# Moving fifteen modulation weight tiles from GpSimd to VectorE and TensorE

## The chip, the cores and the metric

The kernel runs on one core of a Trainium2 chip. The core's engines each work through their own instruction list: TensorE (PE in the profile; its weight loads are the row PEld), VectorE (DVE), ScalarE (ACT) and GpSimd (POOL); SyncE (SP) issues transfers. They meet at semaphores. The metric is the device time of one execution in microseconds (us), as the median of several runs.

## What is computed

One encoder block on 256 tokens of width 1024, in float32: a mixer of two kinds of attention and then a retrieval of experts, each between a norm with modulation and a gate. Cut to what matters here:

```
c_act = silu(c)                                   # c: 1024 numbers
ada = c_act @ w_ada + b_ada                       # 1024 x 6144
shift1, scale1, gate1, shift2, scale2, gate2 = split(ada, 6)
h = rms_norm(x, norm1_g) * (1 + scale1) + shift1
proj = h @ w_in                                   # queries, keys, values of both groups
mixed = [rms_norm(windowed attention), rms_norm(neighbourhood attention)]
x = x + gate1 * (mixed @ w_out)
h2 = rms_norm(x, norm2_g) * (1 + scale2) + shift2
x = x + gate2 * peer(h2, w_query, sub_keys, u_experts, v_experts)
return rms_norm(x, final_g)
```

The six modulation vectors have 1024 entries each, and each entry is a sum over 1024 products of silu(c) with a column of w_ada.

## The kernel before

All channels lie on the partitions, eight chunks of 128, and the 256 tokens along the free dimension. The kernel has two large stages.

**The first stage** covers everything from the first norm to the first queries of the expert part. It is not written in the order in which it runs. Its code records jobs (`add`), each with one or more engines that could do it, a cost in microseconds for each, what it waits for, and the buffers that it takes and frees. `run_plan` at the end of the stage then searches 300 rounds for an order by these costs, and writes out one instruction list per engine from the best one. The search starts from a fixed seed (`SEED = 729`). So a different cost, or a job on another engine, can change the order of everything in the stage, and which engine does a job that has more than one alternative.

The jobs that matter here:

- `load` (L586): SyncE loads weight tiles of 128 x 1024 f32 one after another, in the order in which they are recorded, into nine early buffers and eight raw ones that are taken in turn. A transfer waits until its buffer has been freed.
- `load_ada` (L592): forty modulation tiles, eight chunks of 128 channels for each of scale1, shift1, gate1, shift2 and scale2. A tile holds the 128 output channels on its partitions and the 1024 inputs along its rows. For 25 of them VectorE multiplies the tile by silu(c), which lies on all partitions as `ca`, and sums each row in the same instruction (`scalar_tensor_tensor` with an accumulator, L606). For the 15 in `ON_POOL` GpSimd multiplies (L598) and ScalarE then sums the rows (L601). Gate2's eight tiles are read later, in the second stage.
- `load_w` (L614): a weight of the projections is split into a rounded high half (ScalarE) and a low half, the rest (`low`, L630: VectorE, or GpSimd as the second alternative, because `LO_POOL` is 1). Products with it are three passes (L442).
- attention units 0 to 7: scores on PE (L925, L927), bias and maximum on VectorE (L945), exponentials on ScalarE (L949), small additions for the sink (L962), multiplication by the reciprocal of the sum (L982: VectorE, ScalarE or GpSimd), transposes on PE (L999, L1002), copies of these (L1007 on VectorE, L1009 on ScalarE), the outputs on PE (L1021, L1025), scaling by the group norm's weight (L1032 VectorE, L1034 ScalarE). Evacuations of the input projection are L851 and L870.
- `op` (L540) is a helper for small elementwise jobs, so that many different ones carry that line; the low halves of activations (`hb`) are among them.
- the output projection in two groups of four weight tiles (first units 0 to 3, then 4 to 7), each followed by the gate (L1077) and the residual addition (L1081); then the second norm, and the early queries on PE (L1113).

**The second stage** has the rest of the queries, the top-k and the expert tables: products with the u table (L1507), then with the v table (L1557), and rows gathered by index (L1421) that VectorE multiplies and adds (L1443). Its tiles come through SyncE (L373) into the same raw buffers and others.

Of the kernel before, what the change touches and what calls it, by code (L numbers as in the profile page):

```python
# [12 lines left out]
AF = mybir.ActivationFunctionType  # L13
# [3 lines left out]
P = 128  # L17
D = 1024
NC8 = 8
# [16 lines left out]
NCST = _o  # L36

SHIFT1, SCALE1, GATE1, SHIFT2, SCALE2, GATE2 = range(6)
ON_POOL = {(GATE1, 0), (GATE1, 2), (GATE1, 3), (GATE1, 5), (GATE1, 7), (SCALE2, 0), (SCALE2, 1), (SCALE2, 2), (SCALE2, 4), (SCALE2, 5), (SCALE2, 6), (SHIFT2, 1), (SHIFT2, 2), (SHIFT2, 3), (SHIFT2, 4)}
RAW = 4  # L40
SETTLE = 6.0
SETS = (64, 32)
# [17 lines left out]
LO_POOL = 1  # L60
# [5 lines left out]
def kernel(ctx: ExitStack, tc: tile.TileContext, xT, crow, vecs, cst, w_ada, w_in, w_out,  # L66
# [78 lines left out]
    def add(alts, *deps, take=(), free=(), lag=0.0, after=None, rows=P):  # L145
        return Job(alts, deps, take, free, lag, after, rows)
# [174 lines left out]
    MM = 0.1095  # L321
# [16 lines left out]
    tiles = {}  # L338
# [178 lines left out]
    def silu(y, x):  # L517
        S.activation(y, x, AF.Exp, scale=-1.0)
        V.tensor_scalar(y, y, 1.0, None, op0=ALU.add)
        V.reciprocal(y, y)  # L520
        V.tensor_mul(y, y, x)

    silu(c8t[:8], c8[:8])
    for w, part in ((0, SCALE1), (1, SCALE2)):
        a0 = VEC["b_ada"][0] + part * 8
        V.scalar_tensor_tensor(gb[:, w, :], vec[:, a0:a0 + 8], 1.0, v_("g2" if w else "g1"),
                               op0=ALU.add, op1=ALU.mult)
# [64 lines left out]
    def load_ada(part, c):  # L592
        key = ("ada", part, c)
        m = load(w_ada[part, c], key)
        col = ada[:, part, c:c + 1]
        if (part, c) in ON_POOL:
            def mul():
                G.tensor_mul(tiles[key], tiles[key], ca)  # L598

            def total():  # L600
                S.activation(tiles[key], tiles[key], AF.Copy, accum_out=col)  # L601

            m = add([("pool", 2.3, mul)], m, *cas)
            column[part, c] = add([("act", 1.04, total)], m, free=[key])
        else:
            column[part, c] = add([("dve", 1.15, lambda: V.scalar_tensor_tensor(  # L606
                tiles[key], tiles[key], 1.0, ca, op0=ALU.mult, op1=ALU.mult, accum_out=col))], m, *cas, free=[key])

    halved = {}
# [4 lines left out]
    def load_w(kind, i):  # L614
        key = ("w", kind, i)
        m = load(SRC[kind][i], key)
        hkey = ("h", kind, i)
        held_key[kind, i] = hkey
        if (kind, i) in WHOLE or kind == "q" and i < NQ:
            halved[kind, i] = whole[kind, i] = m  # L620
            held_key[kind, i] = key
            return

        def high():
            halves[kind, i] = new_halves(got(hkey))
            S.activation(halves[kind, i][0], tiles[key].rearrange("p (c n) -> p c n", n=P), AF.Copy)

        def low(e):
            hi, lo = halves[kind, i]
            e.tensor_sub(lo, tiles[key].rearrange("p (c n) -> p c n", n=P), hi.bitcast(F32))  # L630

        a = add([("act", 0.95, high)], m, take=[("split", hkey)])
        halved[kind, i] = add([("dve", 1.14, lambda: low(V))] + [("pool", 2.3, lambda: low(G))] * LO_POOL, a, free=[key])


    lscr = dram.tile([8, 512], F32, name="lscr")
# [1001 lines left out]
def _layout(np, i):  # L1638
# [26 lines left out]
    for c in range(8 if KT == 16 else 0):  # L1665
# [5 lines left out]
    w_out = w_out.reshape(2, 4, P, 4, 2, P).transpose(0, 3, 2, 4, 1, 5).reshape(8, P, D)  # L1671
    rpb = np.stack([i["rpb_b"][0].reshape(4, 2, 465)[:, :, 108 + 31 * r:264 + 31 * r] for r in range(4)])
    rpb = rpb.transpose(2, 0, 1, 3).reshape(-1)
    return {
        "xT": i["x"][0].T.reshape(8, P, T).transpose(1, 0, 2),
        "crow": i["c"].reshape(8, P),
        "vecs": vec,
        "cst": _constants(np),
        "w_ada": i["w_ada"][0].T.reshape(6, 8, P, D),
        "w_in": w_in,  # L1680
        "w_out": w_out,
        "w_query": tiles(i["w_query"][0]),
# [27 lines left out]
```

## Time and profile before

| | |
|---|---|
| median of 3 runs | 851.04 us (849.75 to 851.42) |
| profiled execution | 850.8 us, of it 849.0 us between the first and the last instruction (the span) |
| PE busy | 775.2 us, 91% of the span |
| VectorE busy | 593.1 us, 70% |
| GpSimd busy | 330.6 us, 39% |
| ScalarE busy | 268.0 us, 32% |
| mean granted clock of TensorE | 0.976 |

A share over the whole span is an average over stages with different limits, so it does not say what sets the time of one of them. The rows below take the span in stretches: up to 61 us, to 141.5 and to 176.3 us lie in the first stage (61 us is the end of the products for the first twelve column blocks of the input projection, 141.5 us the beginning of the second half of the output projection, 176.3 us the end of the early queries), from 220 us the products with the u table, from 482.3 us those with the v table.

Names in the rows: `big`, `raw` and `vec` are areas in SBUF, `b` a PSUM bank, `xs` the residual, `hi`/`lo` the halves of a weight, `hb` the halves of activations, `in_...` tensors in memory.

### The profile page before, as it was taken

The page shows a single profiled execution, that of the slowest core. Times are in us where ns is not written, and L with a number is a line of the kernel's source. Part 1 is how long each engine was busy: PE and PEld are TensorE (multiplying, and loading weights), DVE is VectorE, ACT ScalarE, POOL GpSimd, SP SyncE. Part 2 cuts the span into 40 slices and gives each one's busy share as a digit, 9 for nine tenths or more (in the row PEclk, how much of TensorE's full clock was granted, in tenths as well). Part 3 has the DMA queues.
Part 4 walks back from the last instruction along what each step waited for, and adds up shares of the span by engine and source line. Part 5 has one row for each costly group of instructions (what it writes and reads, how often), then busy time and mean ns, then how long its engine had stood idle before and what let it go on. Part 6 is the DMA issues. An engine that isn't in the chain of part 4 may idle for free.

```text
span 849.0 us, 15375 instructions
## 1 busy us (share of the span) xinstructions
PE 775.2 (91%) x5846; PEld 753.9 (89%) x5846; DVE 593.1 (70%) x1308; ACT 268.0 (32%) x741; POOL 330.6 (39%) x271
## 2 busy tenths in 40 slices
PE   3998786789799999999999999999999989899894
PEld 1997575689799999999999999999999988899893
DVE  6999999887677999569998775644435444453534
ACT  4456675456231112179876521000000000000003
POOL 2545686456314436412233233533333333332300
PEclk9999998999999999999999999999999999999997
DMA  8995666095768999999999999999999999999951
GB/s 328 408 328 206 223 227 234 0 348 202 259 229 297 392 413 395 416 413 361 359 378 374 401 371 416 415 412 416 415 416 415 414 415 416 415 413 418 414 205 50
DMA packets 81212, 289.27 MB, mean 341 GB/s; under 512 B 9281, under 2 KB 10825, under 8 KB 81010
## 3 DMA queue, kind: packets, MB, share of 16 engines
q1 hardware_dynamic: 36352, 125.60, 38.5%
q0 software_dynamic: 27776, 100.79, 30.2%
q10 hardware_dynamic: 17010, 61.89, 18.4%
q8 instruction: 46, 0.75, 0.4%
q14 instruction: 28, 0.23, 0.1%
HBM read 287.18 MB, written 1.07 MB: 340 GB/s over the span
## 4 chain that ended last, share of the span: by engine, by line
PE 34%; DMA 28%; issue 5%; DVE 3%; POOL 3%; ACT 0%; DVEq 0%; ACTq 0%; POOLq 0%
PE b L1507 27%; DMA row<-in_vE,big 24%; PE b L1557 4%; DMA raw<-in_vE,big 3%; PE b L1474 2%; DVE accg L1443 1%; POOL row L1421 1%; DMA row<-in_uT 1%; POOL raw L1421 1%; DMA row<-in_vE 1%; PE b L1342 1%; PE b L1562 0%; POOL big L1421 0%; DVE big L1443 0%; POOL lo L398 0%
## 5 line engine op out<-in xcount | busy, mean ns | idle before, releaser
L1507 PE MATMUL b<-big 128*128 128x160 f32 x928 | 134.3, 302 | 4.0 <-ACT big L1489 4.0
L1557 PE MATMUL b<-big 128*128 128x160 f32 x944 | 131.0, 299 | 5.0 <-DMA big<-in_vE 4.2
L1557 PEld LDWEIGHTS b<-big 128*128 128x128 f32 x944 | 129.0, 190 | 5.7 <-DMA big<-in_vE 4.7
L1557 PE MATMUL b<-big,row 128*128 128x160 f32 x864 | 125.5, 305 | 7.4 <-DMA row<-in_vE 7.4
L1507 PEld LDWEIGHTS b<-big 128*128 128x128 f32 x928 | 128.4, 191 | 4.2 <-ACT big L1489 4.2
L1557 PEld LDWEIGHTS b<-big,row 128*128 128x128 f32 x864 | 121.8, 194 | 8.1 <-DMA row<-in_vE 4.3
L1507 PE MATMUL b<-big,row 128*128 128x160 f32 x752 | 106.6, 300 | 0.0
L1507 PEld LDWEIGHTS b<-big,row 128*128 128x128 f32 x752 | 103.0, 190 | 0.0
L540 ACT ACTIVATE big<-xs 128x256 f32<-128x256 f32 (+1 forms) x20 | 9.1, 457 | 283.8 <-DVE xs L540 273.8
L1421 POOL DMA_INDIRECT row<-in_vE,big x48 | 49.9, 1039 | 88.0 <-DVE accg L1443 58.5
L1443 DVE SCALAR_TENSOR_TENSOR accg<-row,big,accg 128x1024 f32<-128x1024 f32 x32 | 41.2, 1286 | 51.2 <-DMA row<-in_vE,big 48.4
L442 PE MATMUL b<-hb,hi 128*128 128x256 f32 x432 | 65.5, 295 | 1.9 <-DVE hb L540 1.9
L1421 POOL DMA_INDIRECT raw<-in_vE,big x36 | 37.2, 1033 | 70.5 <-DVE accg L1443 45.5
L1421 POOL DMA_INDIRECT row<-in_uE,big x37 | 39.6, 1071 | 61.9 <-DVE big L1493 29.2
L1489 ACT ACTIVATE big<-b 128x160 f32<-128x160 f32 (+23 forms) x110 | 29.0, 266 | 104.3 <-PE b L1507 85.4
L442 PEld LDWEIGHTS b<-hb,hi 128*128 128x128 f32 x432 | 58.2, 199 | 3.9 <-DVE hb L540 2.1
L1421 POOL DMA_INDIRECT raw<-in_uE,big x34 | 34.5, 1015 | 63.6 <-DVE raw L1434 29.0
L1443 DVE SCALAR_TENSOR_TENSOR accg<-raw,big,accg 128x1024 f32<-128x1024 f32 x23 | 29.6, 1285 | 38.2 <-DMA raw<-in_vE,big 38.1
L1465 ACT ACTIVATE oh<-iota,ebf 128x128 f16<-128x128 f16 x160 | 51.0, 394 | 13.2 <-PE b L1474 9.4
L1421 POOL DMA_INDIRECT big<-in_uE,big x25 | 25.7, 1028 | 70.1 <-issue 29.3
L442 PE MATMUL b<-hb,lo 128*128 128x256 f32 x216 | 33.1, 291 | 6.6 <-DVE lo L630 5.0
L442 PEld LDWEIGHTS b<-hb,lo 128*128 128x128 f32 x216 | 28.7, 194 | 8.6 <-DVE lo L630 5.6
(212 smaller groups left out, 1381.2 us busy)
## 6 DMA issues: line engine op xcount, KB each, us to landing
big<-in_uT SPq DMA_DIRECT2D x36, 512.0 KB
big<-in_w_ada SPq DMA_DIRECT2D x33, 512.0 KB
big<-in_vE SPq DMA_DIRECT2D x31, 512.0 KB
row<-in_vE SPq DMA_DIRECT2D x29, 512.0 KB
big<-in_vE ACTq DMA_DIRECT2D x28, 512.0 KB
row<-in_vE ACTq DMA_DIRECT2D x25, 512.0 KB
row<-in_uT ACTq DMA_DIRECT2D x24, 512.0 KB
row<-in_uT SPq DMA_DIRECT2D x23, 512.0 KB
```

Source lines behind the costliest of these rows:

```text
L442: PE.matmul(ps, w[:, wc, :], r[:, rc, :], start=(n == 0), stop=(n == last))
L540: return (e, cost, lambda: f(*a, **k))
L1342: PE.matmul(px[:, c * P:(c + 1) * P], rep[:, 4 * i + c, :], ident, start=True, stop=True)
L1421: G.indirect_dma_start(row, None, uE if k < GT else vE, bass.IndirectOffsetOnAxis(ap=cidx[:, k % GT:k % GT + 1], axis=0))
L1443: V.scalar_tensor_tensor(accg[w], row, ag[:, k - GT:k - GT + 1], accg[w], op0=ALU.mult, op1=ALU.add)
L1465: S.activation(oh1[:, k, :], iota1, AF.Square, scale=-1.0, bias=ebf[:, t0 + k:t0 + k + 1])
L1474: PE.matmul(pg[:, k, :], pr[:, i, :, k], oh1[:, k, :], start=(i == 0), stop=(i == 1))
L1489: S.activation(gz[:, e, t:], ps[:, 0, t:ND], AF.Gelu_apprx_tanh)
L1507: PE.matmul(ps[:, 0, 0:ND], w[:, c, :], h2[:, c, GT:], start=(c == 0), stop=(c == NC8 - 1))
L1557: PE.matmul(acc[c][:, 0, GT:], w[:, c, :], gz[:, e, :], start=(e == 0), stop=(e == NE - 1), skip_group_check=True)
```

## The change

The set `ON_POOL` and its branch go. Five of its fifteen tiles (four of scale2, one of shift2) are in a new set `ON_PE`. For them the host lays the tile out the other way, with 128 inputs on the partitions and eight blocks of 128 output channels; PE takes each block as the stationary operand and multiplies it by one column of silu(c) in column form (`cs`, made by a second `silu` at the start), eight matmuls that add up in one PSUM bank, and ScalarE copies the resulting column of 128 numbers to its place. These jobs wait for their tile's transfer and for a free bank. The other ten tiles fall into the branch for VectorE. Two costs of the planner are raised, 1.15 to 1.3 us for VectorE's sum and 1.14 to 1.22 for VectorE's low half. In the changed kernel most lines are one or two higher (L540 is L541, L630 is L632, L1081 is L1083), VectorE's sum is L608 and the new product L602.

```diff
@@ -36,7 +36,7 @@
-ON_POOL = {(GATE1, 0), (GATE1, 2), (GATE1, 3), (GATE1, 5), (GATE1, 7), (SCALE2, 0), (SCALE2, 1), (SCALE2, 2), (SCALE2, 4), (SCALE2, 5), (SCALE2, 6), (SHIFT2, 1), (SHIFT2, 2), (SHIFT2, 3), (SHIFT2, 4)}
+ON_PE = {(SCALE2, 0), (SCALE2, 2), (SCALE2, 4), (SCALE2, 6), (SHIFT2, 2)}
@@ -521,6 +521,7 @@
     silu(c8t[:8], c8[:8])
+    silu(cs, v_("c"))
@@ -593,17 +594,18 @@
         col = ada[:, part, c:c + 1]
-        if (part, c) in ON_POOL:
-            def mul():
-                G.tensor_mul(tiles[key], tiles[key], ca)
-
-            def total():
-                S.activation(tiles[key], tiles[key], AF.Copy, accum_out=col)
-
-            m = add([("pool", 2.3, mul)], m, *cas)
-            column[part, c] = add([("act", 1.04, total)], m, free=[key])
+        if (part, c) in ON_PE:
+            def products_c():
+                w = tiles[key].rearrange("p (c n) -> p c n", n=P)
+                pc = take_bank(("adac", part, c))
+                for k in range(NC8):
+                    PE.matmul(pc[:, 0, 0:1], w[:, k, :], cs[:, k:k + 1], start=(k == 0), stop=(k == NC8 - 1))
+
+            m = add([("pe", 16 * MM, products_c)], m, take=[("bank", ("adac", part, c))], free=[key])
+            column[part, c] = add([("act", 0.25, lambda: S.activation(
+                col, tiles["adac", part, c][:, 0, 0:1], AF.Copy))], m, free=[("adac", part, c)])
         else:
-            column[part, c] = add([("dve", 1.15, lambda: V.scalar_tensor_tensor(
+            column[part, c] = add([("dve", 1.3, lambda: V.scalar_tensor_tensor(
                 tiles[key], tiles[key], 1.0, ca, op0=ALU.mult, op1=ALU.mult, accum_out=col))], m, *cas, free=[key])
@@ -630,7 +632,7 @@
-        halved[kind, i] = add([("dve", 1.14, lambda: low(V))] + [("pool", 2.3, lambda: low(G))] * LO_POOL, a, free=[key])
+        halved[kind, i] = add([("dve", 1.22, lambda: low(V))] + [("pool", 2.3, lambda: low(G))] * LO_POOL, a, free=[key])
@@ -1671,12 +1673,15 @@
+    ada = i["w_ada"][0].T.reshape(6, 8, P, D).copy()
+    for part, c in ON_PE:
+        ada[part, c] = ada[part, c].T.reshape(8, P, P).transpose(1, 0, 2).reshape(P, D)
...
-        "w_ada": i["w_ada"][0].T.reshape(6, 8, P, D),
+        "w_ada": ada,
```

The order of the instructions is drawn up anew from the changed jobs. On GpSimd, in the middle of the first stage (L660 is the last step of the neighbourhood's bias; `raw_...` are buffers of the loads), stood before:

```order
L660 TENSOR_TENSOR big<-big 128x4x128 x3
L598 TENSOR_TENSOR big<-big 128x1024 x2
L598 TENSOR_TENSOR raw_667<-raw_667,big 128x1024
L598 TENSOR_TENSOR raw_724<-raw_724,big 128x1024
L598 TENSOR_TENSOR big<-big 128x1024
L982 TENSOR_TENSOR big<-big 128x2x256 x2
L598 TENSOR_TENSOR raw_884<-raw_884,big 128x1024
L598 TENSOR_TENSOR big<-big 128x1024 x3
L540 TENSOR_TENSOR big<-big 128x256
L982 TENSOR_TENSOR big<-big 128x2x256
```

and there stands after the change:

```order
L662 TENSOR_TENSOR big<-big 128x4x128 x3
L632 TENSOR_TENSOR lo_662<-big,hi_661 128x1024
L632 TENSOR_TENSOR lo_761<-raw_722,hi_760 128x1024
L632 TENSOR_TENSOR lo_888<-raw_818,hi_887 128x1024
L984 TENSOR_TENSOR big<-big 128x2x256
L632 TENSOR_TENSOR lo_977<-big,hi_976 128x1024
L541 TENSOR_TENSOR big<-big 128x256
L541 TENSOR_TENSOR hb<-big,hb 128x256
L541 TENSOR_TENSOR big<-big 128x256
L541 TENSOR_TENSOR hb<-big,hb 128x256 x2
```

The fifteen multiplications are gone from there, and four low halves stand in their place, with the weighing of attention weights (L982, now L984) later than before.

On PE, around the first attention units (`b_...` are PSUM banks, L442 products of the input projection, L862 and L999 transposes, L925 scores; `hi`, `lo` with a number the halves of one weight tile), stood before:

```order
L999 MATMUL b_824<-big 128x128 x4
L999 MATMUL b_833<-big 128x128 x4
L925 MATMUL b_841<-big 128x256
L925 MATMUL b_842<-big 128x256
L925 MATMUL b_841<-big 128x256
L925 MATMUL b_842<-big 128x256
L442 MATMUL b_858<-hb,hi_803 128x256 x8
L442 MATMUL b_858<-hb,lo_804 128x256 x8
L442 MATMUL b_858<-hb,hi_803 128x256 x8
L999 MATMUL b_899<-big 128x128 x4
L1021 MATMUL b_906<-big 64x256 x4
L442 MATMUL b_917<-hb,hi_853 128x256 x8
```

and now, around the first of the new products:

```order
L442 MATMUL b_862<-hb,hi_848 128x256 x8
L442 MATMUL b_862<-hb,lo_849 128x256 x8
L442 MATMUL b_862<-hb,hi_848 128x256 x8
L1001 MATMUL b_902<-big 128x128 x4
L602 MATMUL b_908<-cs,big 128x1 x8
L864 MATMUL b_930<-big 128x128 x4
L1001 MATMUL b_937<-big 128x128 x4
L927 MATMUL b_946<-big 128x256
L927 MATMUL b_947<-big 128x256
L927 MATMUL b_946<-big 128x256
L927 MATMUL b_947<-big 128x256
L1001 MATMUL b_962<-big 128x128 x4
```

The new product (L602) stands between the transposes of one unit and those before the scores of the next, and the products of the column blocks ahead of it come before the scores rather than after them.

On VectorE, in the second half of the output projection (L1077 gates, L1081 adds to the residual), stood before:

```order
L1081 TENSOR_TENSOR xs<-xs,big 128x256
L630 TENSOR_TENSOR lo_1408<-big,hi_1407 128x1024
L721 TENSOR_TENSOR big<-big 128x256
L715 TENSOR_SCALAR big<-b_1372 128x256
L724 TENSOR_TENSOR big<-big 128x256
L727 SCALAR_TENSOR_TENSOR big<-big 128x256
L1077 SCALAR_TENSOR_TENSOR big<-b_1381,ada,big 128x256
L1081 TENSOR_TENSOR xs<-xs,big 128x256
L1077 SCALAR_TENSOR_TENSOR big<-b_1426,ada,big 128x256
L1077 SCALAR_TENSOR_TENSOR big<-b_1381,ada,big 128x256
L1081 TENSOR_TENSOR xs<-xs,big 128x256 x2
L1077 SCALAR_TENSOR_TENSOR big<-b_1426,ada,big 128x256
```

and now (L1079 and L1083 are the same steps):

```order
L1079 SCALAR_TENSOR_TENSOR big<-b_1435,ada,big 128x256
L1083 TENSOR_TENSOR xs<-xs,big 128x256
L1079 SCALAR_TENSOR_TENSOR big<-b_1435,ada,big 128x256
L632 TENSOR_TENSOR lo_1494<-raw_1211,hi_1493 128x1024
L1079 SCALAR_TENSOR_TENSOR big<-b_1468,ada,big 128x256 x2
L1083 TENSOR_TENSOR xs<-xs,big 128x256 x2
L632 TENSOR_TENSOR lo_1533<-big,hi_1532 128x1024
L1079 SCALAR_TENSOR_TENSOR big<-b_1505,ada,big 128x256
L1083 TENSOR_TENSOR xs<-xs,big 128x256
L1079 SCALAR_TENSOR_TENSOR big<-b_1505,ada,big 128x256
L1083 TENSOR_TENSOR xs<-xs,big 128x256
L632 TENSOR_TENSOR lo_1570<-big,hi_1569 128x1024
```

Three low halves of weights now stand between the gates and the residual additions, where one stood before, ahead of the norm's steps (L715 to L727).

## Rows read from the trace of the kernel before

**Rows 1.** Stretches: length, busy us (instructions) per engine, PE clock, DMA share, GB/s.

```profile
0.00:61.00 61.00, 45.35 (x308) 42.15 (x308) 52.40 (x84) 29.17 (x46) 26.11 (x24) 1.00 0.95 359
61.00:141.50 80.50, 59.58 (x505) 50.01 (x503) 79.69 (x154) 53.05 (x140) 55.87 (x25) 0.95 0.66 233
141.50:176.30 34.80, 28.45 (x154) 25.47 (x155) 31.66 (x59) 17.83 (x40) 17.04 (x16) 0.84 0.20 67
220.00:482.30 262.30, 256.88 (x2045) 254.91 (x2044) 213.96 (x629) 121.02 (x400) 89.42 (x84) 0.99 0.95 366
482.30:797.00 314.70, 302.35 (x2217) 300.83 (x2216) 157.95 (x183) 15.15 (x52) 111.08 (x110) 0.99 1.02 411
```

**Rows 2.** VectorE's groups, 61 to 141.5 us: busy us, mean ns, idle before.

```profile
L606 DVE SCALAR_TENSOR_TENSOR raw<-raw,big 128x1024 f32<-128x1024 f32 x6 | 14.6, 2435 | 0.0
L630 DVE TENSOR_TENSOR lo<-raw,hi 128x1024 fp32r<-128x1024 f32 x7 | 13.3, 1903 | 0.0
...
L982 DVE TENSOR_TENSOR big<-big 128x512 f32<-128x512 f32 x9 | 9.7, 1085 | 0.2
L630 DVE TENSOR_TENSOR lo<-big,hi 128x1024 fp32r<-128x1024 f32 x4 | 7.1, 1768 | 0.0
L606 DVE SCALAR_TENSOR_TENSOR big<-big 128x1024 f32<-128x1024 f32 x3 | 5.4, 1796 | 0.0
L962 DVE TENSOR_TENSOR big<-big,vec 128x2 f32<-128x2 f32 x8 | 4.8, 631 | 0.0
L540 DVE TENSOR_TENSOR hb<-big,hb 128x256 fp32r<-128x256 f32 x3 | 3.9, 1309 | 0.0
L1007 DVE COPY big<-b 128x512 f32<-128x512 f32 x4 | 2.6, 676 | 0.0
...
L851 DVE TENSOR_SCALAR big<-b 128x256 f32<-128x256 f32 x6 | 2.4, 413 | 0.0
L1032 DVE TENSOR_SCALAR big<-b,vec 128x256 f32<-128x256 f32 x5 | 2.4, 471 | 0.0
...
L870 DVE COPY big<-b 128x512 f32<-128x512 f32 (+1 forms) x3 | 1.8, 592 | 0.0
```

**Rows 3.** Single instructions of VectorE, GpSimd idle: start us, length us.

```profile
76.04 0.28 DVE L962 TENSOR_TENSOR big<-big,vec 128x2 f32<-128x2 f32 x2
...
83.06 1.22 DVE L630 TENSOR_TENSOR lo<-big,hi 128x1024 fp32r<-128x1024 f32 x1
...
84.67 1.22 DVE L606 SCALAR_TENSOR_TENSOR big<-big 128x1024 f32<-128x1024 f32 x1
85.81 0.08 DVE L606 DVE_READ_ACCUMULATOR big<-big 128x1 f32 x1
...
86.55 0.69 DVE L982 TENSOR_TENSOR big<-big 128x512 f32<-128x512 f32 x1
...
139.88 0.41 DVE L540 TENSOR_TENSOR hb<-big,hb 128x256 fp32r<-128x256 f32 x1
```

**Rows 4.** GpSimd's groups, 61 to 141.5 us.

```profile
L598 POOL TENSOR_TENSOR big<-big 128x1024 f32<-128x1024 f32 x11 | 32.0, 2933 | 4.9 <-DMA big<-in_w_ada 4.9
L598 POOL TENSOR_TENSOR raw<-raw,big 128x1024 f32<-128x1024 f32 x4 | 11.5, 2882 | 0.0
...
L630 POOL TENSOR_TENSOR lo<-raw,hi 128x1024 fp32r<-128x1024 f32 x1 | 2.4, 2372 | 0.0
```

**Rows 5.** Single instructions of PE, same columns as rows 3.

```profile
115.53 0.69 PE L1025 MATMUL b<-big 128*64 128x64 f32 x16
...
177.36 1.05 PE L1358 MATMUL b<-big 128*128 128x128 f32 x8
```

**Rows 6.** PE's waits, 61 to 141.5 us: waited for, total us, times, longest.

```profile
PE b L442 <- DVE lo L630: 5.0, 3, 2.2
```

**Rows 7.** Waits of SP's own queue, 20 to 180 us, same columns.

```profile
SPq L373 <- PE b L1113: 30.0, 1, 30.0
SPq L586 <- DVE lo L630: 26.9, 11, 4.8
```

## The prediction

> **What bounds the kernel now.** I read the table of stretches first [rows 1]. The reader is to see one engine without a gap: from 61 to 141.5 us VectorE is busy 79.7 of 80.5 us, while PE is busy 59.6, ScalarE 53.1 and the DMA engines only 0.66 of their time. So in this stretch, which runs from the end of the first twelve column blocks of the input projection to the second half of the output projection, VectorE sets the pace. Before it the DMA share is 0.95 and VectorE is nearly full too. After it (141.5 to 176.3 us) stands a chain on which no engine is full: the rest of the output projection, residual, norm, first queries. From 220 us on PE (256.9 of 262.3), and from 482 us on the DMA engines (share 1.02), are full.
>
> Then I asked why VectorE is full. The groups of its instructions in that stretch [rows 2] show the same operation at very different lengths: the modulation sum (L606) takes 2.435 us on average over six and 1.796 over three, the low half of a weight (L630) 1.903 and 1.768, an addition of two columns (L962) 0.631. The single instructions [rows 3] show what they take when GpSimd is idle beside them: 1.22, 1.22, and 0.14 (0.28 for two). GpSimd's groups in the stretch [rows 4] name the neighbour: 43.5 of its 55.9 busy us [rows 1, 4] are the fifteen multiplications that the change takes away. VectorE loses time when GpSimd works on two operands beside it.
>
> The excess, group by group against the undisturbed length: L606 6 x 1.215 + 3 x 0.576 = 9.0; L630 7 x 0.683 + 4 x 0.548 = 7.0; L982 9 x 0.395 = 3.6; L962 8 x 0.491 = 3.9; L540 on hb 3 x 0.899 = 2.7. Together **26.2 us**, or 0.47 us per busy us of GpSimd.
>
> **The change part by part.**
> *GpSimd's fifteen multiplications go.* Their share of the excess is 26.2 x 43.5 / 55.9 = 20.4 us of VectorE's time, all inside the stretch.
> *Ten of them become VectorE instructions* of the form that is there already: 1.22 + 0.08 for reading the accumulator [rows 3], 1.30 x 10 = 13.0 us. They land in the stretch as well; the order of VectorE shows 19 such sums there where there were nine.
> *The schedule is drawn anew, and moves other work.* By the order, VectorE gives up to ScalarE four copies L1007 (2.7), three L870 (1.8), five scalings L1032 (2.4), three of the evacuations L851 (3 x 0.41 = 1.2) and three multiplications L982 (3 x 0.69 = 2.1): 10.2 us [rows 2, 3]. Of the low halves, three fewer are on VectorE in the stretch (3.7 us), and GpSimd has three more there, 3 x 2.37 = 7.1 us [rows 4], which cost VectorE 7.1 x 0.47 = 3.3 us of interference.
> *VectorE's sum for the stretch:* 79.7 - 20.4 + 13.0 - 10.2 - 3.7 + 3.3 = **61.7 us**, 18 less than now. The four small operations for the new SiLU of c in columns stand ahead of the first tile, in the front, where VectorE has 8.6 us idle [rows 1], and cost nothing.
> *ScalarE* loses fifteen sums over whole tiles and takes some twenty small instructions; at 53.1 of 80.5 us it hides them.
> *Five tiles go to PE.* Each is eight matmuls of 128x128 f32 weights on one column. No such operation is in this trace. An f32 matmul leaves two records (the two scores that the order shows for a step are four in the trace), so a tile is 16 records. Upper bound: the scores L1358 have the same weights with 128 columns, eight records in 1.05 us [rows 5], 2.1 us a tile, 10.5 us for five. Lower bound: L1025 has half the weight columns and 64 columns, 16 records in 0.69 us [rows 5], 0.7 us a tile, 3.5 us for five; less than nothing is excluded, since PE gives nothing up. I take the upper end, whose weights are the same. All five stand in the stretch in PE's order, between the attention units.
> Here a page adds a figure. The Trainium skill (TensorE: Matmul & The Clock Gate, section LDWEIGHTS) gives the time of a weight load as columns / 1.2 ns; an estimate from it is 107 ns for each of the 80 loads, 8.5 us, and PE's sum would be 68.1 instead of the one below. No run here shows such a load alone.
> *PE's sum for the stretch:* 59.6 + 10.5 = **70.1 us**, or 63.1 at the lower price. So the bound changes hands: VectorE needs 61.7, PE 63 to 70. What is late next is PE, which stands in order: a product waits for its own tile's transfer, and behind it stand the transposes and scores of the next attention unit, for which VectorE and ScalarE wait. Today PE is idle 20.9 of the 80.5 us, and its largest named wait is for VectorE's low halves (5.0 us in three waits) [rows 6]; such waits shrink when VectorE runs faster, but not to nothing. I take 70.1 us: it is PE's sum at the upper price without waits, or at the lower price with 7 us of them, a third of today's. The stretch gets **10.4 us** shorter.
> *The tail.* Between 141.5 and 176.3 us VectorE gets three low halves more, among the residual additions: 3 x 1.22 = 3.7 us at worst on the path. GpSimd loses three there (3 x 2.37 = 7.1 us), and at the 0.47 above VectorE gets 3.3 us back. I take 0, ends -2 and +4.
> *The front* (to 61 us) has no multiplication on GpSimd; 0.
> *All the rest* moves forward as a block. The loads of the query and expert tiles wait 30.0 us for PE's early queries L1113 [rows 7], the last step of the first stage, so they start earlier by what that stage saves, and nothing later waits on a fixed time.
>
> **Sum** against the profiled execution's own 850.8 us (span 849.0; the median of the runs is 851.04, 0.2 above it): 850.8 - 10.4 + 0 = 840.4, so **840 us**.
>
> A rule of the Trainium skill that speaks against the change: Vector Engine (DVE) Microarchitecture Reference, section Points that are easy to get wrong, says that a scalar_tensor_tensor with two SBUF sources that are not bf16 runs at half throughput. The undisturbed L606 takes 1.22 us [rows 3], no longer than the plain subtraction L630 on as many elements, so the trace does not bear it out.
>
> **The rivals.**
> 1. *PE is the light one* (0.7 us a tile) and waits little: the stretch falls to 63.1, 17.4 us less: 833; with the tail's -2, 831. For it: VectorE is 99% busy now in the same order of work. Against: it wants PE to lose nearly all its waits.
> 2. *A smaller gain: the upper price and 8 us of waits on PE*: the stretch is 78.1, the time 848. For it: the waits of one attention unit for the next are not VectorE's throughput alone. Against: PE's largest named wait ends with VectorE [rows 6].
> 3. *Slower: PE's waits do not shrink.* If they come from each unit's chain (scores, VectorE, ScalarE, transposes) and from the new waits for transfers rather than from VectorE's throughput, the stretch is 59.6 + 20.9 + 10.5 = 91.0, 10.5 longer: 861 us. It decides from 10.4 us of waits on (80.5 - 59.6 - 10.5), half of today's. For it: SP's queue waits 26.9 us for VectorE's low halves before it can load [rows 7], so tiles do come late. Against: the same row says that it is VectorE that holds the loads.
> 4. *No change: the first stage gets shorter and the gain is lost later*, because the second stage is held by its transfers alone: 850.8. Against: those transfers are released by the first stage [rows 7], and from 220 us on PE is full, not waiting for them [rows 1].
> 5. *The ten new sums take twice as long as those that are there*, 10 x 1.22 us more on VectorE: 61.7 + 12.2 = 73.9 us is then the bound, the gain 6.6, the time 844. The undisturbed L606 [rows 3] speaks against it. This is what the page's rule above would make of the change.
>
> **How the numbers follow.** Forecast (gain 4 to 15 us, 836 to 847): 0.57. Rival 1: 0.12. Rival 2 (847 to 849.3): 0.10. Rival 5: 0.01. Rival 4 and an even balance, within 0.2% of the median (849.3 to 852.7): 0.08. Slower, rival 3: 0.12. A measurement of this kernel can tell about 0.2%, 1.7 us, from no change. So faster 0.80, same 0.08, slower 0.12. The range 831 to 852 reaches from PE's lower price with the better tail to no gain at all; it leaves out rival 3 and a little at both ends.
>
> **What would show each step.** In the profile after, VectorE's L608 sums (35 of them) should be near 1.22 us in the median and few above 2; GpSimd busy some 43 us less in the first 180 us. The products L602 should take 0.7 to 2.1 us a tile. The second half of the output projection should start at about 131 us instead of 141.5, and the expert stage some ten us sooner. That stage should keep its pace. Wrong would be: sums still at 2 us (the interference had another source), PE waiting over 10 us in the stretch for transfers or for its neighbours (rival 3), or an early first stage with the expert stage starting no sooner (rival 4).

## The result

The changed kernel takes **841.23 us** (median of 4 runs, 840.5 to 842.69) against 851.0 for the kernel before beside it (849.75 to 851.42): the ratio is 0.989, with an interval of 0.9872 to 0.9908. The forecast was 840, its range 831 to 852. The sign and the size hold. The way there holds only in part: the stretch that was to give 10.4 us gave 7.3, and the front and the tail, both put at 0, moved by +6.4 and -7.7 us and nearly offset each other.

| | before | after |
|---|---|---|
| profiled execution, its span | 850.8, 849.0 | 840.7, 838.9 |
| PE busy | 775.2 (91%) | 782.1 (93%) |
| VectorE busy | 593.1 (70%) | 573.2 (68%) |
| ScalarE busy | 268.0 (32%) | 263.0 (31%) |
| GpSimd busy | 330.6 (39%) | 300.9 (36%) |
| mean granted clock | 0.976 | 0.972 |

The prediction's stretches were cut at fixed times [rows 1]. To compare two kernels, the cuts have to be at the same piece of work. Below, the stretches of both end at: the last product of the first twelve column blocks; the beginning of the second half of the output projection; its end; the end of the early queries. The columns are those of [rows 1]. Before:

```profile
0.00:61.25 61.25, 45.60 (x310) 42.26 (x310) 52.65 (x84) 29.37 (x47) 26.36 (x24) 1.00 0.95 359
61.25:143.04 81.79, 60.84 (x506) 51.13 (x507) 80.98 (x155) 54.36 (x144) 57.06 (x26) 0.94 0.66 232
143.04:156.36 13.32, 13.32 (x98) 13.02 (x96) 13.05 (x23) 5.24 (x9) 7.67 (x6) 0.88 0.10 36
156.36:170.83 14.47, 10.02 (x38) 7.94 (x38) 11.60 (x24) 8.44 (x21) 5.61 (x5) 0.88 0.00 1
```

After:

```profile
0.00:67.62 67.62, 47.64 (x310) 44.47 (x311) 54.43 (x85) 27.37 (x42) 30.18 (x25) 0.92 0.90 337
67.62:142.11 74.49, 69.57 (x588) 61.49 (x586) 66.58 (x161) 52.26 (x147) 27.24 (x19) 0.91 0.72 251
142.11:153.97 11.86, 11.86 (x99) 11.83 (x98) 10.23 (x21) 8.21 (x18) 4.62 (x4) 1.00 0.12 37
153.97:162.16 8.19, 8.10 (x36) 6.39 (x35) 5.98 (x14) 3.11 (x8) 1.01 (x2) 1.00 0.38 141
```

| stretch | before | after | difference | predicted |
|---|---|---|---|---|
| front | 61.25 | 67.62 | +6.4 | 0 |
| attention units, first half of the output projection | 81.79 | 74.49 | -7.3 | -10.4 |
| second half of the output projection | 13.32 | 11.86 | -1.5 | 0 |
| residual, norm, early queries | 14.47 | 8.19 | -6.3 | with the row above |
| all the rest, to the end of the span | 678.2 | 676.7 | -1.4 | 0 |
| span | 849.0 | 838.9 | -10.1 | -10.4 |

In the second stretch the reader sees the bound change hands as forecast: VectorE was full (80.98 of 81.79) and now has 7.9 us idle; PE now lacks 4.9 us of being full, where 21.0 were idle before (2.5 of the 4.9 are a wait for GpSimd's L541; before the transposes L1001 stand 2.3 for which the profile names no releaser). VectorE's groups in the stretch from 67.62 to 142.11 us, to be held against [rows 2], are these:

```profile
L608 DVE SCALAR_TENSOR_TENSOR big<-big 128x1024 f32<-128x1024 f32 x10 | 15.1, 1518 | 0.0
L608 DVE SCALAR_TENSOR_TENSOR raw<-raw,big 128x1024 f32<-128x1024 f32 x9 | 12.0, 1347 | 0.0
L984 DVE TENSOR_TENSOR big<-big 128x512 f32<-128x512 f32 x6 | 6.4, 1063 | 0.2
L632 DVE TENSOR_TENSOR lo<-raw,hi 128x1024 fp32r<-128x1024 f32 x4 | 6.3, 1563 | 0.1
L632 DVE TENSOR_TENSOR lo<-big,hi 128x1024 fp32r<-128x1024 f32 x4 | 5.3, 1324 | 0.8 <-ACT hi L628 0.8
L1079 DVE SCALAR_TENSOR_TENSOR big<-b,ada,big 128x256 f32<-128x256 f32 x8 | 3.5, 477 | 0.9 <-PE b L442 0.8
...
L964 DVE TENSOR_TENSOR big<-big,vec 128x2 f32<-128x2 f32 x8 | 1.5, 217 | 0.0
```

There are 19 sums now, as the order said, and their mean has gone from 2.435 and 1.796 us to 1.347 and 1.518; the small additions went from 0.631 to 0.217 us. The five tiles on PE, single instructions as in [rows 5]:

```profile
92.96 1.84 PE L602 MATMUL b<-cs,big 128*128 128x1 f32 x16
...
108.94 3.41 PE L602 MATMUL b<-cs,raw 128*128 128x1 f32 x16
...
116.79 1.95 PE L602 MATMUL b<-cs,big 128*128 128x1 f32 x16
...
132.60 1.84 PE L602 MATMUL b<-cs,raw 128*128 128x1 f32 x16
...
139.97 1.95 PE L602 MATMUL b<-cs,big 128*128 128x1 f32 x16
```

Together 11.0 us, where the upper price gave 10.5. Each is 16 records long, as assumed. The one of 3.41 us ran while the granted clock was at the lower of its two levels (0.58 on average from 108 to 112 us).

**Where the front lost 6.4 us.** PE's waits up to 68 us for the modulated input (`hb`), before 7.6 us in one wait, are now:

```profile
PE b L808 <- ACT hb L541: 14.4, 3, 6.8
```

A column block's product waits for a chain: two sums on VectorE, two small operations on the 128 numbers (scale and shift), ScalarE's modulation, and then PE. On VectorE these small operations are, among their neighbours:

```profile
32.29 0.14 DVE L541 TENSOR_TENSOR ada<-ada,vec 128x1 f32<-128x1 f32 x1
...
40.74 1.22 DVE L608 SCALAR_TENSOR_TENSOR big<-big 128x1024 f32<-128x1024 f32 x1
...
41.89 2.34 DVE L541 SCALAR_TENSOR_TENSOR mod<-ada,vec,gb 128x1 f32<-128x1 f32 x1
...
51.09 0.21 DVE L541 SCALAR_TENSOR_TENSOR mod<-ada,vec,gb 128x1 f32<-128x1 f32 x1
...
55.26 1.35 DVE L541 SCALAR_TENSOR_TENSOR mod<-ada,vec,gb 128x1 f32<-128x1 f32 x1
56.53 1.21 DVE L632 TENSOR_TENSOR lo<-raw,hi 128x1024 fp32r<-128x1024 f32 x1
57.66 1.32 DVE L541 TENSOR_TENSOR ada<-ada,vec 128x1 f32<-128x1 f32 x1
```

and on GpSimd, at the same time, stand a low half that the new order has put there and the neighbourhood's bias:

```profile
40.84 3.38 POOL L632 TENSOR_TENSOR lo<-big,hi 128x1024 fp32r<-128x1024 f32 x1 [1.10 <-ACT hi L628]
...
54.20 7.17 POOL L662 TENSOR_TENSOR big<-big 128x512 f32<-128x512 f32 x3
```

An operation on one column takes 0.14 to 0.21 us in the front while GpSimd is idle. Here it takes 2.34, 1.35 and 1.32, and in the last case the order also put a low half between the two that the chain needs. In all three cases the small operation ends together with the GpSimd instruction beside it: at 44.23 us (the low half at 44.22), at 56.61 and at 58.98 (the first two of the bias's three steps, read singly, at 56.57 and 58.96). VectorE's sum that had begun at 40.74, 0.10 us before the low half, kept its 1.22 us. So in these rows a small operation waited for the end of the GpSimd instruction, however short it was itself. The last block's modulation on ScalarE began at 59.02 us, in the kernel before at 54.08:

```profile
54.08 0.60 ACT L540 ACTIVATE big<-big,ada,mod 128x256 f32<-128x256 f32 x1 [2.10 <-DVE ada L540]
```

```profile
59.02 0.60 ACT L541 ACTIVATE big<-big,ada,mod 128x256 f32<-128x256 f32 x1 [3.85 <-DVE ada L541]
```

These waits are not the whole loss. PE's idle time in the front grew by 4.3 us; the other 2.0 us are the same 310 matmul records at a lower granted clock (47.64 us busy instead of 45.60). The clock fell after a slice in which PE had little to do:

```profile
56.00:60.00 4.00, 0.93 (x8) 0.73 (x7) 4.00 (x4) 0.95 (x3) 4.00 (x3) 1.00 0.57 197
60.00:64.00 4.00, 3.88 (x21) 3.89 (x22) 2.79 (x3) 1.23 (x3) 1.37 (x1) 0.61 0.58 206
```

**Where the tail gained 7.7 us.** VectorE's last rows before the norm's refinement, in the kernel before:

```profile
163.48 0.42 DVE L540 TENSOR_TENSOR big<-big 128x256 f32<-128x256 f32 x1
166.58 0.42 DVE L715 TENSOR_SCALAR big<-b 128x256 f32<-128x256 f32 x1 [2.67 <-ACT big L712]
```

and after:

```profile
156.08 1.41 DVE L541 TENSOR_TENSOR big<-big 128x256 f32<-128x256 f32 x3 [0.21 <-ACT big L541]
159.22 0.42 DVE L717 TENSOR_SCALAR big<-b 128x256 f32<-128x256 f32 x1 [1.73 <-ACT big L714]
```

Before, PE was done with the output projection at 156.36 us, and VectorE needed 7.5 us more (to 163.90) for gates, additions and squares that were still queued. After, PE is done at 153.97 and VectorE 3.5 us later. VectorE's backlog was not paid off at 141.5 us, where the prediction's stretch ended; it was carried into the tail. This is 4.0 of the 7.7 us. Another 2.4 are PE's clock. In the kernel before, PE waited twice for VectorE around the second half of the output projection, and not at all there after the change:

```profile
PE b L750 <- DVE big L540: 7.6, 2, 4.1
```

After each of these waits the granted clock stood near its lower level (0.58 from 143.04 to 147.00 us, 0.50 from 163.90 to 166.58), and the same products took 1.5 us longer in the second half and 0.9 in the norm. The last 1.3 us are early queries: from the norm's L715 on (L717 after the change) PE had 21 matmul records left before, 14 after.

### The profile page after: what moved, and what is told of

Read it like the earlier page. It is cut to its first block, busy times and chain, and to the rows that moved or that the text cites. A ratio compares the mean times of both kernels' runs of the same rounds, so it can differ in the third digit from the quotient of the medians.

```text
span 838.9 us, 15523 instructions
## 1 busy us (share of the span) xinstructions
PE 782.1 (93%) x5926; PEld 763.1 (91%) x5926; DVE 573.2 (68%) x1307; ACT 263.0 (31%) x738; POOL 300.9 (36%) x262
## 3 DMA queue, kind: packets, MB, share of 16 engines
q10 hardware_dynamic: 17010, 61.89, 18.6%
## 4 chain that ended last, share of the span: by engine, by line
PE 40%; DMA 24%; issue 4%; DVE 3%; POOL 2%; ACT 0%; ACTq 0%; DVEq 0%; POOLq 0%
PE b L1509 27%; DMA raw<-in_vE,big 19%; PE b L1559 10%; DMA big<-in_vE,big 2%; PE b L1476 2%; POOL row L1423 1%; DVE accg L1445 1%; DMA row<-in_uT 1%; DMA row<-in_vE 1%; DMA big<-in_vE 1%; POOL raw L1423 1%; PE b L1344 0%; PE b L1564 0%; POOL big L1423 0%; DVE big L406 0%
## 5 line engine op out<-in xcount | busy, mean ns | idle before, releaser
L1559 PE MATMUL b<-big 128*128 128x160 f32 x944 | 132.6, 301 | 10.5 <-DMA big<-in_vE 9.7
L1559 PEld LDWEIGHTS b<-big 128*128 128x128 f32 x944 | 130.4, 192 | 11.5 <-DMA big<-in_vE 10.5
L1509 PE MATMUL b<-big 128*128 128x160 f32 x928 | 135.6, 303 | 3.8 <-ACT big L1491 3.8
L1509 PEld LDWEIGHTS b<-big 128*128 128x128 f32 x928 | 129.6, 193 | 4.0 <-ACT big L1491 4.0
L1559 PE MATMUL b<-big,row 128*128 128x160 f32 x864 | 121.9, 300 | 0.8 <-DMA row<-in_vE 0.7
L1559 PEld LDWEIGHTS b<-big,row 128*128 128x128 f32 x864 | 118.4, 190 | 1.2 <-DMA row<-in_vE 1.2
L1509 PE MATMUL b<-big,row 128*128 128x160 f32 x752 | 106.6, 300 | 0.0
L1509 PEld LDWEIGHTS b<-big,row 128*128 128x128 f32 x752 | 103.0, 190 | 0.0
L541 ACT ACTIVATE big<-xs 128x256 f32<-128x256 f32 (+1 forms) x20 | 9.1, 457 | 276.0 <-DVE xs L541 270.7
L442 PE MATMUL b<-hb,hi 128*128 128x256 f32 x432 | 62.4, 287 | 0.0
L442 PEld LDWEIGHTS b<-hb,hi 128*128 128x128 f32 x432 | 55.6, 191 | 1.0 <-issue 0.7
L1467 ACT ACTIVATE oh<-iota,ebf 128x128 f16<-128x128 f16 x160 | 51.0, 394 | 12.9 <-PE b L1476 11.3
L808 PE MATMUL b<-hb,hi 128*128 128x256 f32 x192 | 29.1, 308 | 14.4 <-ACT hb L541 14.4
L808 PEld LDWEIGHTS b<-hb,hi 128*128 128x128 f32 x192 | 27.4, 216 | 15.6 <-ACT hb L541 15.6
```

What stands on the lines that cost most here:

```text
L442: PE.matmul(ps, w[:, wc, :], r[:, rc, :], start=(n == 0), stop=(n == last))
L541: return (e, cost, lambda: f(*a, **k))
L808: PE.matmul(tiles["acc", n // 2][:, n % 2, :], w[:, b, :], r[:, c, :], start=(c == 0 and t == 0 and n % 2 == 0), stop=(c == NC8 - 1 and t ...
L1467: S.activation(oh1[:, k, :], iota1, AF.Square, scale=-1.0, bias=ebf[:, t0 + k:t0 + k + 1])
L1509: PE.matmul(ps[:, 0, 0:ND], w[:, c, :], h2[:, c, GT:], start=(c == 0), stop=(c == NC8 - 1))
L1559: PE.matmul(acc[c][:, 0, GT:], w[:, c, :], gz[:, e, :], start=(e == 0), stop=(e == NE - 1), skip_group_check=True)
```

## The experiments

The theory: GpSimd's multiplications made VectorE's instructions long, VectorE's work set the length of the first stage, and PE is the bound after the change. The rivals: a luckier order, the five tiles on PE as the real gain, or tiles on PE that cost nothing. For each kernel I read the stretch up to the end of its early queries; the first two columns come from that row of its trace, the idle time is their difference. Ratios are to runs of the kernel before that were taken beside each kernel.

| kernel | VectorE busy | end of early queries | VectorE idle | median us | ratio to before, interval |
|---|---|---|---|---|---|
| before | 158.3 | 170.8 | 12.6 | 851.0 | |
| e1, costs only | 158.5 | 170.6 | 12.1 | 849.3 | 0.9991 (0.9972 to 1.0011) |
| e9, before, start 1 | 157.0 | 174.2 | 17.2 | 855.4 | 1.006 (1.0041 to 1.008) |
| e2, same order | 154.5 | 166.6 | 12.0 | 845.5 | 0.9946 (0.9925 to 0.9967) |
| e3, no multiplications | 138.2 | 151.1 | 12.9 | 830.0 | 0.9746 (0.971 to 0.9781) |
| e4, all on VectorE | 144.5 | 157.6 | 13.2 | 837.9 | 0.9859 (0.982 to 0.9899) |
| e10, the same, start 1 | 151.1 | 165.0 | 13.9 | 844.9 | 0.9941 (0.992 to 0.9963) |
| e11, the same, start 2 | 140.7 | 155.5 | 14.8 | 836.7 | 0.9844 (0.982 to 0.987) |
| after | 137.2 | 162.2 | 24.9 | 841.2 | 0.989 (0.9872 to 0.9908) |
| e5, lighter tiles on PE | 136.5 | 155.0 | 18.6 | 835.4 | 0.9823 (0.98 to 0.9846) |
| e6, tiles on PE twice | 138.2 | 179.8 | 41.6 | 858.6 | 1.0091 (1.0069 to 1.0112) |
| e7, after, start 1 | 140.0 | 156.7 | 16.7 | 834.5 | 0.9817 (0.98 to 0.9833) |
| e8, after, start 2 | 140.8 | 158.4 | 17.6 | 835.9 | 0.982 (0.9796 to 0.9843) |
| e12, e7 without low halves on GpSimd | 135.6 | 153.6 | 18.1 | 831.5 | 0.9781 (0.9759 to 0.9803) |

The column of idle times carries the main reading. Wherever no modulation tile is on PE, with the one exception of e9, the stage ends 12 to 15 us after VectorE's busy time is used up, whether that is 138 or 158 us: VectorE's work sets the stage's length. With tiles on PE, VectorE idles for 17 us or more. The gap between the two groups is narrow at starts 1 and 2 (13.9 and 14.8 us against 16.7 and 17.6), and why e9 has 17.2 stays open.

### e1: the two costs alone

```diff
-            column[part, c] = add([("dve", 1.15, ...
+            column[part, c] = add([("dve", 1.3, ...
-        halved[kind, i] = add([("dve", 1.14, ...
+        halved[kind, i] = add([("dve", 1.22, ...
```

> The kernel before, with only the two raised costs of the planner (1.3 and 1.22 us); the fifteen multiplications stay on GpSimd, but the order is drawn up anew. Theory (the gain of 9.8 us comes from taking the multiplications off GpSimd): the long sums and low halves on VectorE stay long (excess over their undisturbed lengths near 46 us up to the end of the early queries), and the time stays within about 4 us of before: 847 to 855 us. Rival (the gain is a luckier order, which any new costs could have brought): 845 us or less.

Measured: 849.3 us, the ratio's interval holds 1. This new order brings nothing. But the order moves the front here too: it ends at 66.38 us, 5.1 later than before, with no work moved, and the stage still ends at the same time, since VectorE's sum is the same.

### e2: the order kept, the multiplications on VectorE

```diff
             def mul():
-                G.tensor_mul(tiles[key], tiles[key], ca)
+                V.scalar_tensor_tensor(tiles[key], tiles[key], 1.0, ca, op0=ALU.mult, op1=ALU.mult, accum_out=col)
             def total():
-                S.activation(tiles[key], tiles[key], AF.Copy, accum_out=col)
+                pass
```

> The order of the kernel before is kept; at the place where GpSimd multiplied, VectorE does product and sum in one instruction, and ScalarE's fifteen sums are gone. Theory (prices as in the prediction): VectorE gets back 20.4 us of interference and takes 15 x 1.30 = 19.5 us, so its sum hardly moves and so does the time: 846 to 853 us; with the multiplications gone the mean of the sums is near 1.3 us. Rival A (the interference is worth more than the overlap shows): 840 to 845. Rival B (VectorE's queue now holds sums that wait for transfers, with everything behind them waiting): over 855.

Measured: 845.5 us, between the theory's bounds and rival A's upper end (a gain of 4 us, not 1). The stretch up to the end of the early queries:

```profile
0.00:166.58 166.58, 129.45 (x948) 113.13 (x948) 154.54 (x313) 81.92 (x188) 53.28 (x46) 0.95 0.68 249
```

VectorE's busy time is 3.7 us shorter (158.27 before), and the stage ends 4.3 us sooner. With the interference of e3 below (20.1 us) the fifteen sums cost 20.1 - 3.7 = 16.4 us, 1.1 each; the prediction took 1.30, because it added the reading of the accumulator (0.08), which overlaps, to a length of 1.22 that itself overlaps the next instruction. In the trace of after two sums in a row start 1.15 us apart (98.20 and 99.35 us). Waiting sums in VectorE's queue (rival B) did no harm.

### e3: the multiplications left out

```diff
             def mul():
-                G.tensor_mul(tiles[key], tiles[key], ca)
+                pass
```

> The order of the kernel before; GpSimd's fifteen multiplications are left out, ScalarE still sums the (unmultiplied) tiles. Measures the disputed cost by itself. Theory: VectorE gives up 20 us in the stretch from the end of the first twelve column blocks to the second half of the output projection, PE becomes the bound there with some of its waits, and the stretch loses 10 to 18 us: 832 to 841 us. Rival (GpSimd's multiplications cost VectorE little, its slow instructions have another source): 846 us or more, and sums on VectorE still near 2 us.

Measured: 830.0 us, a ratio of 0.9746, 19.7 us less than the kernel before beside it (849.7) and beyond the lower bound of 832. Stretch and groups (from 60.42 to 121.59 us, the same work as [rows 2]):

```profile
0.00:151.05 151.05, 123.14 (x948) 109.46 (x948) 138.20 (x282) 95.79 (x218) 55.56 (x45) 0.98 0.76 275
```

```profile
L630 DVE TENSOR_TENSOR lo<-raw,hi 128x1024 fp32r<-128x1024 f32 x7 | 9.3, 1334 | 0.7 <-ACT hi L626 0.7
L606 DVE SCALAR_TENSOR_TENSOR raw<-raw,big 128x1024 f32<-128x1024 f32 x6 | 8.7, 1445 | 0.0
...
L606 DVE SCALAR_TENSOR_TENSOR big<-big 128x1024 f32<-128x1024 f32 x3 | 3.6, 1211 | 0.0
L962 DVE TENSOR_TENSOR big<-big,vec 128x2 f32<-128x2 f32 x8 | 0.9, 154 | 0.0
```

The same instructions in the same order: 1.903 to 1.334, 2.435 to 1.445, 1.796 to 1.211, 0.631 to 0.154 us. VectorE's busy time falls by 158.27 - 138.20 = **20.1 us**; the prediction said 20.4. The time falls by nearly as much (19.7; the end of the early queries by 19.8). So the interference had lain on the path almost in full. PE, busy 123.14 of 151.05 us, did not become the bound here, since it has no modulation tiles to take.

### e4, e10 and e11: all fifteen on VectorE

```diff
-ON_PE = {(SCALE2, 0), (SCALE2, 2), (SCALE2, 4), (SCALE2, 6), (SHIFT2, 2)}
+ON_PE = set()
```

e10 and e11 start the planner's search elsewhere as well (`SEED = 1`, `SEED = 2`).

> The changed kernel with the five tiles of TensorE on VectorE too, so all fifteen there; order drawn up anew. Theory (VectorE and PE are near balance after the change): VectorE takes 5 x 1.30 = 6.5 us more, PE 11 us less (five tiles took 11.0 us in the changed kernel), VectorE is the bound again at about 73 us in that stretch, which lasted 74.5: 838 to 845 us. Rival (the gain hangs on the five tiles on TensorE): 846 us or more.

> All fifteen tiles on VectorE, starting point 1; to be compared with the changed kernel at the same starting point (834.5 us). Theory (near balance: VectorE takes five sums of 1.15 us more, 5.7 us, and PE gives up the 5.8 us that the five tiles cost on its path): 832 to 838 us. Rival A (the tiles on TensorE are the dearer place, through the clock they lower): 831 us or less. Rival B (VectorE is the tighter bound): 839 us or more.

> As the run before with starting point 2; to be compared with the changed kernel at 2 (835.9 us). Theory (near balance): 833 to 839 us. Rival A (TensorE the dearer place): 832 us or less. Rival B (VectorE the tighter bound): 840 us or more.

Measured: 837.9, 844.9 and 836.7 us; the changed kernel at the same three starting points has 841.2, 834.5 and 835.9. e4 ends just under its range (838). The rival that the gain hangs on the tiles on PE falls with e4. Which place is better for the five does not show: the sign changes with the order. e10 lies where its rival B put it, but hardly for rival B's reason, VectorE's five sums, since these are in e11 too. What sets it apart in the traces is the number of low halves on GpSimd; that these are the cause was not tried by itself. They are, in e10, up to the end of the early queries:

```profile
L632 POOL TENSOR_TENSOR lo<-big,hi 128x1024 fp32r<-128x1024 f32 x6 | 18.0, 3003 | 8.3 <-ACT hi L628 8.3
L632 POOL TENSOR_TENSOR lo<-raw,hi 128x1024 fp32r<-128x1024 f32 x4 | 12.4, 3114 | 20.3 <-ACT hi L628 17.6 <-issue 2.7
```

Ten, 30.4 us, where e4 and e11 have five (13.0 and 14.6 us). In e4:

```profile
L632 POOL TENSOR_TENSOR lo<-big,hi 128x1024 fp32r<-128x1024 f32 x4 | 10.6, 2671 | 23.7 <-ACT hi L628 14.6 <-PE b L927 9.1
L632 POOL TENSOR_TENSOR lo<-raw,hi 128x1024 fp32r<-128x1024 f32 x1 | 2.4, 2367 | 13.7 <-PE b L442 13.7
```

VectorE has five low halves fewer than in e4 and is still busy 6.6 us longer.

### e5 and e6: how much of the tiles on PE is on the path

e5 keeps one of a tile's eight products; e6 makes all eight twice and halves the sum:

```diff
-                for k in range(NC8):
-                    PE.matmul(pc[:, 0, 0:1], w[:, k, :], cs[:, k:k + 1], start=(k == 0), stop=(k == NC8 - 1))
+                PE.matmul(pc[:, 0, 0:1], w[:, 0, :], cs[:, 0:1], start=True, stop=True)
```

```diff
-                for k in range(NC8):
-                    PE.matmul(pc[:, 0, 0:1], w[:, k, :], cs[:, k:k + 1], start=(k == 0), stop=(k == NC8 - 1))
+                for n in range(2 * NC8):
+                    k = n % NC8
+                    PE.matmul(pc[:, 0, 0:1], w[:, k, :], cs[:, k:k + 1], start=(n == 0), stop=(n == 2 * NC8 - 1))
```

> The changed kernel in its own order, with seven of the eight products of each of the five tiles on TensorE left out (one 128-row block of the inputs is summed). PE gives up about 9.6 of the 11.0 us that the five tiles took. Theory A (PE is the bound of the stretch after the change, as the prediction has it): most of that comes off the time, 831 to 836 us. Theory B (VectorE's work and the chains between the engines set the time, the products lie in PE's idle time): 839 to 842 us.

> The changed kernel in its own order, each of the five tiles' eight products made twice into the same sum, which ScalarE halves when it copies the column. PE gets 11 us more. Theory A (PE is the bound): 849 to 853 us. Theory B (the products lie in PE's idle time): under 845 us.

Measured: 835.4 and 858.6 us against 841.2: 5.8 less, 17.3 more. Theory A holds for this order: what the tiles cost PE is on the path after the change, in e5 with 5.8 of some 9.6 us. Whether it acts through PE's time alone was not separated: SP's loads also wait 11.3 us for the buffers that these products free. e5's second stretch, 68.1 us where the changed kernel has 74.5:

```profile
66.86:134.95 68.09, 60.94 (x516) 52.01 (x516) 65.11 (x160) 50.88 (x146) 29.36 (x19) 0.92 0.78 275
```

e6's time is beyond theory A's range (849 to 853), its price higher than the 11 us expected. The second stretch of e6, from 67.35 us, and four slices in it:

```profile
67.35:157.54 90.19, 85.84 (x668) 77.89 (x666) 67.97 (x163) 52.37 (x147) 26.23 (x19) 0.84 0.58 208
```

```profile
120.00:124.00 4.00, 4.00 (x36) 3.17 (x35) 1.71 (x10) 3.17 (x12) 0.00 (x0) 0.81 0.63 239
124.00:128.00 4.00, 4.00 (x24) 4.00 (x25) 2.56 (x7) 1.28 (x7) 0.00 (x0) 0.61 0.02 4
128.00:132.00 4.00, 4.00 (x24) 3.05 (x25) 0.22 (x3) 2.58 (x10) 0.00 (x0) 0.53 0.75 253
132.00:136.00 4.00, 4.00 (x36) 4.00 (x35) 3.93 (x16) 2.14 (x6) 1.93 (x1) 1.00 0.20 52
```

PE is busy 4.00 of 4.00 us in each, and in every slice back to 112 us, and the granted clock still falls to 0.53, during and after a doubled tile (122.81 to 127.92 us); it is at the full level again in the slice in which the output projection's products run (from 131.67 us). The five doubled tiles take 25.5 us instead of 22.0, and what follows them is slow too.

### e7, e8 and e9: other orders

```diff
-    SEED = 729
+    SEED = 1
```

(e8: 2.) e7 and e8 are the changed kernel, e9 is the kernel before.

> The changed kernel with another starting point of the planner's search (1 in place of 729); same jobs, same costs, another order. Theory (the front that became 6.4 us longer is the order's doing, not the moved tiles'): the end of the first twelve column blocks lies somewhere else, 60 to 68 us, and the time follows, 834 to 845 us. Rival (the ten sums on VectorE or the new waits lengthen the front in any order): 66 to 69 us again and 839 to 844 us.

> As the run before, with 2 as the starting point. Theory (order): the front ends between 60 and 68 us, another time again, 834 to 845 us. Rival (moved tiles): 66 to 69 us and 839 to 844 us.

> The kernel before with 1 as the starting point of the planner's search in place of 729. Theory (VectorE's busy time bounds the first stage, and with the multiplications on GpSimd it is long in any order): 845 to 856 us, VectorE busy 155 us or more up to the end of the early queries. Rival (729 is an unlucky order for the kernel before, and part of the gain measured is that): 843 us or less.

Measured: 834.5, 835.9 and 855.4 us. The changed kernel's front ends at 64.21 and 63.76 us in e7 and e8, against 67.62, and in e12 below at 59.95, before the 61.25 of the kernel before: an order can avoid the loss with the tiles moved. Of the two other orders of the kernel before (e1 and e9) neither is faster, so the gain is not bad luck of the start 729; rather the opposite: at start 1 the change is worth 855.4 - 834.5 = 20.9 us, at 729 it is 9.8. All seven whole kernels whose order the planner drew without the multiplications on GpSimd (831.5 to 844.9 us, e12 below among them) lie below all three with them (849.3 to 855.4).

### e12: no low halves on GpSimd

e7's kernel with one number more changed:

```diff
-LO_POOL = 1
+LO_POOL = 0
```

> The changed kernel at starting point 1, with GpSimd no longer offered any low half of a weight: its five (13.4 us on GpSimd) go to VectorE. By the prediction's prices VectorE takes 5 x 1.14 = 5.7 us and gets 13.4 x 0.47 = 6.3 us back: no change beyond the order's own scatter, 832 to 838 us. Rival (a low half on GpSimd costs VectorE more than it saves): 831 us or less. Rival (it costs VectorE little): 839 us or more.

Measured: 831.5 us, 3.0 less than e7, half a microsecond short of the first rival's bound. The intervals of their ratios (0.9759 to 0.9803, 0.98 to 0.9833) hardly touch. e7, then e12, up to the end of the early queries:

```profile
0.00:156.69 156.69, 134.05 (x1026) 120.18 (x1026) 139.98 (x284) 91.32 (x214) 56.85 (x47) 0.96 0.77 278
```

```profile
0.00:153.60 153.60, 131.74 (x1027) 120.30 (x1028) 135.55 (x291) 89.29 (x211) 45.45 (x45) 0.97 0.76 280
```

VectorE took five low halves more (5 x 1.14 = 5.7 us) and is busy 4.4 us less than in e7 (139.98). So 13.4 us of low halves on GpSimd had cost it 10.1 us, 0.75 for each microsecond; e10 against e4 gives about the same, (6.6 + 5.7) / 17.4 = 0.71. The prediction used 0.47, a mean over all of GpSimd's work. Both pairs differ in order too, so this is an estimate. It is the fastest kernel that computes the whole block, and faster than both kernels of this case.

## Why the prediction was right, step by step

- **GpSimd's interference, 20.4 us: right**, 20.1 in e3 up to the end of the early queries.
- **Ten sums at 1.30 us: too dear**, 1.1 to 1.15 (e2). Some 1.5 us. Twice the length (rival 5) shows in no row.
- **Three low halves more on GpSimd at 0.47 us per us: open.** By the estimates from e10 and e12 (0.7 to 0.75) 7.1 us would cost about 5 us and not 3.3. But the rows of the changed kernel's stretch, held against the prediction's undisturbed lengths group by group, leave 9.1 us of excess, as much as the sum left (26.2 - 20.4 + 3.3).
- **VectorE's sum, 18 us less: right in mechanism, not in its place.** In the stretch itself it is 80.98 - 66.58 = 14.4 us less, up to the end of the early queries 158.27 - 137.22 = 21.1. Among what the sum for the stretch left out are gates: eight now run there (3.5 us), three did before.
- **Five tiles on PE at the upper end, 10.5 us: right**, 11.0. The lower clock in one of them was not foreseen.
- **The bound changes hands to PE: right** (e5, e6, both at the start 729). The stretch is 74.5 and not 70.1 us: PE's busy time is as forecast (69.6), but 4.9 us of idle time stay that the sum had left out. Rival 2 (8 us of waits) was half right, rival 3 (no less than today's) is out.
- **The tail, 0: failed.** It gained 7.7 us. The step took a stretch with a full VectorE and let its effect end where the stretch ends. The row for 141.5 to 176.3 us showed VectorE busy 31.66 of 34.80 us [rows 1]: the backlog went on, and with it PE's waits for VectorE and the lower clock after them. What the three low halves that the order had put there cost was not measured apart.
- **The front, 0: failed.** It lost 6.4 us. "No multiplication on GpSimd" said nothing about what a new order would put there: a low half and the bias beside the chain's small operations. Nor did the sum count that PE's clock falls after such a wait (2.0 us). e1 shows 5.1 us lost by the order with no work moved.
- **The rest moves as a block: right**, 1.4 us, within what the orders scatter (674.9 to 679.3 us over all the runs).

Two of the signs that were to show the steps did not come. The second half of the output projection began 0.9 us sooner (142.11 against 143.04) and not some ten, because the front had lost 6.4. And GpSimd was busy 33.7 us less up to the end of the early queries (27.5 less in the first 180 us), not 43. The products with the u table began 7.4 us sooner.

The gain of 10.1 us on the span is -7.3 - 7.7 + 6.4 - 1.4. That it met the forecast's 10.4 owes something to chance: front and tail nearly offset each other. With another start of the search the same forecast would have been 4 to 6 us too high.

## What to carry to other kernels

Where one engine is nearly full through a whole stage, count its work over the stage to the next real wait, not over the stretch in which it is fullest: its backlog runs on into rows that look like a chain. A GpSimd operation on two large operands is to be charged with the time that it takes from VectorE (here 0.5 to 0.75 us per us), in a planner's costs too: an alternative that looks free because GpSimd is idle was worth less than nothing in the one pair that tried it (e7, e12). And where an order is drawn by a search, run more than one start on either side, since here the start alone moved the time by up to 8 us (e10, e11), nearly as much as the change.

## What the runs showed of the hardware

Small operations can suffer as much as large ones: an operation on one column per partition took 2.34 us beside GpSimd's low half, where it takes 0.21 with GpSimd idle, because it ended only with that low half (44.23 and 44.22 us). In the three cases above the small operation lost what was left of the GpSimd instruction beside it, and in a chain such losses add up step by step. And TensorE's granted clock fell during and after long rows of products on a single column although the engine showed no gap: to 0.53 in e6, with PE busy 4.00 of 4.00 us. Elsewhere here it fell after waits (0.61 in the changed kernel's front, after PE had been busy 0.93 of 4.00 us). Whether it is the single column that the clock follows was not tried apart. So moving work of this form to TensorE can cost more than its own 2 us a tile (5.1 instead of 3.7 us for a doubled one).
